# A decoder layer on one core: x and memory also come transposed from the host, factors are applied on the way out

## The chip, the cores and the metric

The kernel runs on one core of a Trainium2 chip. The metric is device time in microseconds (us) of one execution. All arithmetic is in float32; matmuls run on operands split in two parts (hi, lo), so that each product is three matmuls.

## The reference, cut to what matters

One layer of a causal decoder: 1024 tokens of width 1024 (x) and 256 memory tokens of width 1024 (mem). The change touches the two norms at the start and what is made from them:

```python
def rms_norm(x, w):
    y = x * lax.rsqrt(jnp.mean(x * x, axis=-1, keepdims=True) + EPS)
    return y * w

h = rms_norm(x, norm_mix_w)
x = x + hybrid_mixer(h, w_in, pool_w, ...)       # one input projection h @ w_in, two head groups, w_out
h = rms_norm(x, norm_xattn_w)
m = rms_norm(mem, norm_mem_w)
x = x + memory_cross_attention(h, m, wq, wkv, wo) # kv = m @ wkv; k = kv[:, :1024], v = kv[:, 1024:]
h = rms_norm(x, norm_ffn_w)
x = x + conv_ffn(h, w_up, conv_w, conv_b, w_down) # depthwise convolution of width 3, SwiGLU
return rms_norm(x, norm_final_w)
```

The factor of a row (the rsqrt) and the factor of a feature (w) are separate, so that a projection of the unnormalised rows can be multiplied by the row's factor afterwards.

## The kernel before, in words

**Tiling.** Matmuls contract over 128 features at a time, so activations must lie feature-major (features on the partitions). `Feat` (line 230) holds an activation so, in tiles of hi and lo parts; `split` (line 94) makes both: ScalarE writes hi (line 96), VectorE the rest (line 97). Rows come from HBM token-major, are normalised there and transposed by TensorE against an identity, 128x128 at a time (`put_T`, line 302, matmuls of line 307). `norm_feat` (line 312) does that for four tiles of 128 tokens, a block of 512; there are two blocks.

**Norms.** `inv_rms` (line 290) takes the square sum of a row tile on ScalarE (line 292) and the power -0.5 on GpSimd (line 294); `normed` (line 297) multiplies tile, factor and the broadcast norm vector on VectorE (line 299).

**Weights.** Each weight chunk is 512 KB, loaded by SP (`dma`, line 273) and split in two units (`wunit`, lines 117 and 118). A stream takes the units in the order of the jobs, two units ahead. The 16 chunks of the memory projection wkv go to roomy buffers of the pool "big" (40 buffers), so that they can be loaded early; all others go through two raw buffers.

**Jobs.** Matmul work is a list of jobs in fixed order: km (K of memory, 8 blocks of 128 features, each 8 x 3 matmuls 128x256), vm (V of memory, 96 matmuls 128x512), then for each block vg, k, q, r, p, and wout. `fill` runs steps of the first open job for a planned number of us; `weave` runs a chain, such as norm_feat, and fills between its steps. What a chain issues and what jobs issue is ordered for each engine by the program's order and by a planner's estimate of when operands are ready, except for pinned instructions: these stay behind what was traced before them on their engine. All loads by SP are pinned until job vm is done; so are the splits of weights at the start.

**The start** (lines 496 to 523): memory's two row tiles are loaded first, with its norm vector, which TensorE broadcasts with a row of ones (line 502) for the product of line 509; then weight chunks and the four row tiles of x alternate; memory's tiles are transposed. While km and vm run, the first block of x is normalised and transposed, and `make_vec` (line 561) transposes the packed convolution and scale vectors, which five small loads brought (lines 548 to 552). The second block's norm_feat runs beside the output projection of the first (job wout).

Of the kernel before, what the change touches and what calls it, by code (L numbers as in the profile page):

```python
# [8 lines left out]
F32 = mybir.dt.float32  # L9
F32R = mybir.dt.float32r  # L10
AF = mybir.ActivationFunctionType
ALU = mybir.AluOpType
# [3 lines left out]
P = 128  # L16
T = 1024
D = 1024
KT = D // P
TB = 512  # L20
NB = T // TB
M = 256
# [5 lines left out]
HK = KT // 2  # L28
# [11 lines left out]


@with_exitstack
def hybrid_layer(ctx: ExitStack, tc: tile.TileContext, x, mem, norm_mix_w, w_in, pool_w, pool_scale,
                 gk_w2, gk_b, gla_norm_w, w_out, norm_xattn_w, norm_mem_w, wq, wkv, wo,
                 norm_ffn_w, w_up, conv_w, conv_b, w_down, norm_final_w, out):
    nc = tc.nc

    const = ctx.enter_context(tc.tile_pool(name="const", bufs=1))
# [9 lines left out]
    pin = tc.keep_in_program_order  # L58
# [3 lines left out]
    def nm(s):  # L62
        uid[0] += 1
        return f"{s}{uid[0]}"

    def f4(*shape):
        return big.tile([P, *shape], F32, tag="big", name=nm("f"))

    def r4(*shape):
        return big.tile([P, *shape], F32R, tag="big", name=nm("r"))  # L70
# [4 lines left out]
    def sc(n):  # L75
        return small.tile([P, n], F32, tag="small", name=nm("s"))

    def bankA():
        return psA.tile([P, 512], F32, tag="psA", name=nm("pa"))

    def bankB():
        return psB.tile([P, 512], F32, tag="psB", name=nm("pb"))
# [11 lines left out]
    def split(dst, src, scale=None):  # L94
        if scale is None:
            nc.scalar.activation(dst.hi, src, AF.Copy)  # L96
            nc.vector.tensor_tensor(dst.lo, src, dst.hi.bitcast(F32), ALU.subtract)  # L97
        else:
            nc.scalar.activation(dst.hi, src, AF.Copy, scale=scale)
            nc.vector.scalar_tensor_tensor(dst.lo, src, scale, dst.hi.bitcast(F32), ALU.mult, ALU.subtract)  # L100
# [41 lines left out]
    early, issues = [False], []  # L142
# [19 lines left out]
    ws = Stream()  # L162
# [34 lines left out]
    def fill(us):  # L197
        while us > 0:
            c = step()
            if c is None:  # L200
                return
            us -= c
# [6 lines left out]
    def weave(chain):  # L209
        for us in chain:  # L210
            fill(us)
# [8 lines left out]
    def proj_tok(banks, feat, nk, step_k, n):  # L220
        for kc in range(0, nk, step_k // 2):
            w = ws.take()
            for i, ps in enumerate(banks):
                for kk in range(step_k // 2):
                    a = feat.k(kc + kk)
                    mm3(ps, a[:, i * P:(i + 1) * P], w[:, kk, :], kc + kk == 0, kc + kk == nk - 1)
                    yield n * 3 / 2400
# [40 lines left out]
    ident = const.tile([P, P], F32, name="ident")  # L268
# [4 lines left out]
    def dma(dst, src):  # L273
        ins = nc.sync.dma_start(out=dst, in_=src)
        if starting or pinned:
            pin(ins)

    def bcast_row(src, q=nc.gpsimd):
        w = f4(D)
        ins = q.dma_start(out=w, in_=src.partition_broadcast(P))  # L280
        if starting:
            pin(ins)
        return w

    def load_x(t):
        xt = f4(D)
        dma(xt, x[t * P:(t + 1) * P, :])
        return xt

    def inv_rms(xt, junk):  # L290
        ss, rs = sc(1), sc(1)
        nc.scalar.activation(junk, xt, AF.Square, scale=1.0 / 32, accum_out=ss)
        nc.gpsimd.tensor_scalar(ss, ss, EPS, None, ALU.add)
        nc.gpsimd.tensor_tensor(rs, ss, halfneg[:, 0:1], ALU.pow)
        return rs

    def normed(xt, wb, pool=None):
        y = pool.tile([P, D], F32, tag="y", name=nm("y")) if pool else f4(D)
        nc.vector.scalar_tensor_tensor(y, xt, inv_rms(xt, y), wb, ALU.mult, ALU.mult)
        return y  # L300

    def put_T(xn, feat, c0):
        pss = []
        for q in range(2):
            ps = bankB()
            for j in range(4):
                nc.tensor.transpose(ps[:, j * P:(j + 1) * P], xn[:, (4 * q + j) * P:(4 * q + j + 1) * P], ident)  # L307
            pss.append(ps.rearrange("p (k c) -> p k c", k=4))
            feat.put(4 * q, 4, c0, P, pss[q])
        return pss  # L310

    def norm_feat(tiles, wb, feat, lead=6.0):

        ahead = normed(tiles[0](), wb)
        yield lead
        for i in range(len(tiles)):
            xn = ahead
            if i + 1 < len(tiles):
                ahead = normed(tiles[i + 1](), wb)
            put_T(xn, feat, i * P)  # L320
            yield 5.0

    hmix = [None, None]
# [80 lines left out]
    tiles = [0]  # L404
# [34 lines left out]
    att = {}  # L439

    def kmem_evac(f, ps):
        if f == 0:
            att["K"] = Feat(M)
        att["K"].put(f, 1, 0, M, ps.unsqueeze(1))

    def vmem_gen():
        V = att["V"] = [Pair(r4(D), r4(D)) for _ in range(2)]
        for half in range(2):
            banks = [bankA() for _ in range(2)]
            yield from proj_tok(banks, att["m"], KT, 2, 512)  # L450
            for i in range(2):
                split(V[i][:, half * 512:(half + 1) * 512], banks[i])

    hx, oo = [None, None], [None, None]

# [29 lines left out]
    def allow(*keys):  # L485
        for k in keys:
            J[k].open = True


    def load_m(i):  # L490
        mt = f4(D)
        dma(mt, mem[i * P:(i + 1) * P, :])
        return mt

    ones, row = f4(P), f4(D)
    nc.vector.memset(ones[0:1, :], 1.0)
    mts = [load_m(0)]
    dma(row[0:1, :], norm_mem_w.rearrange("(o c) -> o c", o=1))
    mts.append(load_m(1))
    wb_mem = [bankA(), bankA()]  # L500
    for half in range(2):
        nc.tensor.matmul(wb_mem[half], ones[0:1, :], row[0:1, half * 512:(half + 1) * 512], start=True, stop=True)
    att["m"] = Feat(M)
    xn = [f4(D), f4(D)]
    for xt, y in zip(mts, xn):
        rs = inv_rms(xt, y)
        for half in range(2):
            hs = slice(half * 512, (half + 1) * 512)
            pin(nc.vector.scalar_tensor_tensor(y[:, hs], xt[:, hs], rs, wb_mem[half], ALU.mult, ALU.mult))
    for k in range(2):  # L510
        issues[k]()
    ws.load(1)
    xts = [load_x(0)]
    wb_mix = bcast_row(norm_mix_w, nc.sync)
    for i in range(1, 4):
        issues[i + 1]()
        xts.append(load_x(i))
    put_T(xn[0], att["m"], 0)
    ws.load(2)
    put_T(xn[1], att["m"], P)  # L520
    ws.load(2)
    hmix[0] = Feat(TB)


# [7 lines left out]
                            fill=0.0, base=0, channel_multiplier=1)  # L532
# [10 lines left out]
    phalo = mixc.tile([P, 4, HALO], F32, name="phalo")  # L543
    pin(nc.gpsimd.memset(phalo, 0.0))

    rows_a = f4(P)
    rows_b = f4(P)
    pin(nc.sync.dma_start(out=rows_a[0:88, :], in_=conv_w[0:2, :].rearrange("w (f p) -> (w f) p", p=P)))
    pin(nc.sync.dma_start(out=rows_b[0:44, :], in_=conv_w[2, :].rearrange("(f p) -> f p", p=P)))
    pin(nc.sync.dma_start(out=rows_b[44:88, :], in_=conv_b.rearrange("(f p) -> f p", p=P)))  # L550
    pin(nc.sync.dma_start(out=rows_b[88:92, :], in_=pool_scale.rearrange("(f p) -> f p", p=P)))
    pin(nc.sync.dma_start(out=rows_b[92:93, :], in_=gla_norm_w.rearrange("(f p) -> f p", p=P)))
    gkw = mixc.tile([17, 256], F32, name="gkw")
    pin(nc.sync.dma_start(out=gkw[0:16, :], in_=gk_w2))
    pin(nc.sync.dma_start(out=gkw[16:17, :], in_=gk_b.rearrange("(o c) -> o c", o=1)))
    poolw = mixc.tile([P, 4, P], F32, name="poolw")
    pin(nc.sync.dma_start(out=poolw, in_=pool_w.rearrange("g c d -> c g d")))

    vec = const.tile([P, 181], F32, name="vec")

    def make_vec():
        ps = bankB()
        nc.tensor.transpose(ps[:, 0:88], rows_a[0:88, :], ident[0:88, 0:88])
        nc.tensor.transpose(ps[:, 88:181], rows_b[0:93, :], ident[0:93, 0:93])
        nc.vector.tensor_copy(vec, ps[:, 0:181])

    def cw(j, f):
        return vec[:, j * 44 + f:j * 44 + f + 1]
# [129 lines left out]

    starting.clear()
    allow("km", "vm")  # L700
    weave(norm_feat([lambda i=i: xts[i] for i in range(4)], wb_mix, hmix[0], 5.0))
    make_vec()
    finish(J["vm"])
    pinned.clear()
    mixs[0] = Feat(TB)
# [5 lines left out]
    J["wout", 0, 0].limit = None  # L711
    allow(("wout", 0, 0), ("wout", 0, 512))
    hmix[1] = Feat(TB)
    weave(norm_feat([lambda i=i: load_x(4 + i) for i in range(4)], wb_mix, hmix[1]))
    finish(J["q", 1])
    mixs[1] = Feat(TB)
    allow(("r", 1), ("p", 1))
# [162 lines left out]
    for i in range(4):  # L880
# [4 lines left out]
        xn = normed(xres[4 + i], wb_f, ybuf)  # L885
# [302 lines left out]
    for j in list(plan):  # L1188
# [4 lines left out]
    finish(plan[0])  # L1193


_INS = ["x", "mem", "norm_mix_w", "w_in", "pool_w", "pool_scale", "gk_w2", "gk_b", "gla_norm_w", "w_out",
        "norm_xattn_w", "norm_mem_w", "xattn_wq", "xattn_wkv", "xattn_wo", "norm_ffn_w", "ffn_w_up",
        "ffn_conv_w", "ffn_conv_b", "ffn_w_down", "norm_final_w"]


# [18 lines left out]
```

## Time and profile before

| | |
|---|---|
| median of 3 runs | 1299.7 us (1299.69 to 1301.9) |
| profiled execution, its own time | 1303.83 us |
| its span, first to last instruction | 1300.4 us |
| mean granted TensorE clock | 0.994 |
| VectorE busy | 862.9 us (66%) |
| ScalarE busy | 648.7 us (50%) |
| GpSimd busy | 227.7 us (18%) |
| DMA moved | 143.94 MB, mean 111 GB/s |

PE is TensorE's matmuls, PEld its weight loads, DVE VectorE, ACT ScalarE, POOL GpSimd, SPq the sequencer that issues most loads. Matmuls overlap, so the distance between two starts says what one costs in the queue, and the duration says more than that. A tile is named by its variable: `f` and `r` are buffers of the pool "big", `wr`, `wh`, `wl` a raw weight chunk and its two parts, `pa` and `pb` PSUM banks.

### The profile page before, as it was taken

What the parts mean: (1) busy time and instruction counts of PE and PEld (TensorE: products, weight loads), DVE (VectorE), ACT (ScalarE), POOL (GpSimd) and SP (SyncE); (2) the same over time, 40 slices, a digit from 0 to 9 for tenths busy, and PEclk for the clock granted to TensorE, in tenths of its full rate; (3) what the DMA queues carried; (4) which work ended last, traced back from release to release, by engine and by line L of the source; (5) the groups of instructions that cost most, each with busy time, mean ns of one, the idle gap of its engine ahead of it and who ended that gap; (6) DMA issues with size and microseconds to landing.
All of it is one profiled execution on the core that took longest, in us unless ns stands there. A gap on an engine that the chain in (4) does not pass through costs nothing.

```text
span 1300.4 us, 16897 instructions
## 1 busy us (share of the span) xinstructions
PE 1269.9 (98%) x6326; PEld 1059.7 (81%) x6326; DVE 862.9 (66%) x1331; ACT 648.7 (50%) x1169; POOL 227.7 (18%) x238
## 2 busy tenths in 40 slices
PE   8999999999999999999899999999999999999997
PEld 7898878988788889887777888888888886888885
DVE  6723676236757554446887667668667678999865
ACT  6636534364445443335555555545545544474453
POOL 2000110001200000010114443434434420000002
PEclk9999999999999999999999999999999999999999
DMA  9433225332142212233323232232232246875202
GB/s 288 144 101 82 66 98 196 99 81 66 63 148 65 66 52 79 72 117 127 121 68 99 79 98 75 72 98 81 65 97 82 65 149 238 286 249 187 81 22 107
DMA packets 140272, 143.94 MB, mean 111 GB/s; under 512 B 4696, under 2 KB 112926, under 8 KB 140191
## 3 DMA queue, kind: packets, MB, share of 16 engines
q1 hardware_dynamic: 138031, 136.05, 32.5%
q0 software_dynamic: 1584, 5.77, 1.2%
q8 instruction: 49, 0.80, 0.3%
q10 hardware_dynamic: 576, 1.05, 0.2%
q14 instruction: 32, 0.26, 0.1%
HBM read 122.93 MB, written 19.92 MB: 110 GB/s over the span
## 4 chain that ended last, share of the span: by engine, by line
PE 67%; issue 16%; DVE 7%; DMA 4%; ACT 3%; POOL 1%; SPq 0%; POOLq 0%; ACTq 0%; DVEq 0%
PE pa L913 8%; PE pa L914 8%; PE pa L915 8%; PE pa L92 8%; PE pa L90 8%; PE pa L91 8%; PE pb L913 5%; PE pb L914 5%; PE pb L915 5%; DVE r L97 2%; DMA f<-gd 2%; DVE wl L118 1%; PE pb L307 1%; DMA f<-in_norm_ffn_w_dram 1%; DVE wl L97 1%
## 5 line engine op out<-in xcount | busy, mean ns | idle before, releaser
L118 DVE TENSOR_TENSOR wl<-wr,wh 128x512 fp32r<-128x512 f32 (+1 forms) x222 | 152.9, 691 | 208.7 <-ACT wh L117 203.7
L117 ACT ACTIVATE wh<-wr 128x512 fp32r<-128x512 f32 (+1 forms) x222 | 140.0, 632 | 282.9 <-PE pa L91 82.1
L913 PE MATMUL pa<-r,wh 128*128 128x512 f32 x400 | 158.8, 397 | 7.5 <-ACT wh L117 4.5
L90 PE MATMUL pa<-wh,r 128*128 128x512 f32 (+2 forms) x480 | 159.2, 332 | 0.3 <-ACT wh L117 0.3
L915 PE MATMUL pa<-r,wl 128*128 128x512 f32 x400 | 158.6, 397 | 0.0
L914 PE MATMUL pa<-r,wh 128*128 128x512 f32 x400 | 158.4, 396 | 0.0
L91 PE MATMUL pa<-wl,r 128*128 128x512 f32 (+2 forms) x480 | 157.3, 328 | 0.3 <-DVE wl L118 0.3
L92 PE MATMUL pa<-wh,r 128*128 128x512 f32 (+2 forms) x480 | 157.0, 327 | 0.2
L90 PE MATMUL pa<-r,wh 128*128 128x512 f32 (+1 forms) x384 | 149.3, 389 | 0.7 <-ACT r L96 0.7
L92 PE MATMUL pa<-r,wl 128*128 128x512 f32 (+1 forms) x384 | 144.2, 376 | 0.4 <-DVE wl L118 0.3
L91 PE MATMUL pa<-r,wh 128*128 128x512 f32 (+1 forms) x384 | 144.0, 375 | 0.3 <-DVE r L97 0.3
L92 PEld LDWEIGHTS pa<-wh,r 128*128 128x128 f32 x480 | 90.3, 188 | 9.4 <-DVE r L97 1.1
L913 PEld LDWEIGHTS pa<-r,wh 128*128 128x128 f32 x400 | 75.9, 190 | 26.5 <-ACT wh L117 4.7
L90 PEld LDWEIGHTS pa<-wh,r 128*128 128x128 f32 x480 | 90.4, 188 | 8.3 <-ACT wh L117 0.5
L91 PEld LDWEIGHTS pa<-wl,r 128*128 128x128 f32 x480 | 90.4, 188 | 8.2 <-DVE wl L118 0.5
L981 DVE SCALAR_TENSOR_TENSOR f<-f,vec,f 128x1023 f32<-128x1023 f32 x44 | 86.9, 1974 | 14.5 <-ACT f L980 14.5
L915 PEld LDWEIGHTS pa<-r,wl 128*128 128x128 f32 x400 | 75.8, 190 | 17.7 <-DVE wl L118 0.4
L914 PEld LDWEIGHTS pa<-r,wh 128*128 128x128 f32 x400 | 75.9, 190 | 17.0
L117 ACT ACTIVATE wh<-ws 128x512 fp32r<-128x512 f32 x88 | 55.4, 630 | 67.9 <-PE pa L914 33.6
L913 PE MATMUL pb<-r,wh 128*128 128x512 f32 x216 | 85.1, 394 | 0.0
L914 PE MATMUL pb<-r,wh 128*128 128x512 f32 x216 | 85.0, 394 | 0.0
L915 PE MATMUL pb<-r,wl 128*128 128x512 f32 x216 | 84.7, 392 | 0.0
(225 smaller groups left out, 2660.9 us busy)
## 6 DMA issues: line engine op xcount, KB each, us to landing
wr<-in_ffn_w_up_dram SPq DMA_DIRECT2D x47, 512.0 KB, 3.7
wr<-in_ffn_w_down_dram SPq DMA_DIRECT2D x33, 512.0 KB, 3.7
wr<-in_w_in_dram SPq DMA_DIRECT2D x24, 512.0 KB, 4.0
gd<-f SPq DMA_DIRECT2D x22, 512.0 KB, 2.6
f<-gd SPq DMA_DIRECT2D x22, 512.0 KB, 5.8
f<-in_xattn_wkv_dram SPq DMA_DIRECT2D x16, 512.0 KB, 7.6
f<-in_x_dram SPq DMA_DIRECT2D x16, 512.0 KB, 7.6
wr<-in_w_out_dram SPq DMA_DIRECT2D x16, 512.0 KB, 3.6
```

What stands on the lines that cost most here:

```text
L90: nc.tensor.matmul(ps, l.hi, r.hi, start=start, stop=False)
L91: nc.tensor.matmul(ps, l.hi, r.lo, start=False, stop=False)
L92: nc.tensor.matmul(ps, l.lo, r.hi, start=False, stop=stop)
L97: nc.vector.tensor_tensor(dst.lo, src, dst.hi.bitcast(F32), ALU.subtract)
L117: ia = nc.scalar.activation(w.hi, src, AF.Copy)
L118: ib = nc.vector.tensor_tensor(w.lo, src, w.hi.bitcast(F32), ALU.subtract)
L307: nc.tensor.transpose(ps[:, j * P:(j + 1) * P], xn[:, (4 * q + j) * P:(4 * q + j + 1) * P], ident)
L913: nc.tensor.matmul(ps, l.hi, r.hi, start=start, stop=False, **kw)
L914: nc.tensor.matmul(ps, l.hi, r.lo, start=False, stop=False, **kw)
L915: nc.tensor.matmul(ps, l.lo, r.hi, start=False, stop=stop, **kw)
L981: nc.vector.scalar_tensor_tensor(v[:, 1:], u[:, 0:T - 1], cw(1, f), v[:, 1:], ALU.mult, ALU.add)
```

## The change

The host gives three more arrays: x transposed, mem transposed, and `vecs`, in which the convolution and scale vectors and the two norm vectors norm_mix_w and norm_mem_w lie ready as 197 columns of 128 features. The rows of x and mem are still loaded, for their square sums.

- Memory: its transposed features (two loads of 512 KB) are multiplied by norm_mem_w while they are split. K and V are projected from these unnormalised features. V is multiplied by the row factor when it leaves PSUM; for K the factors are a row vector across the free axis, made by `spread_cols` (a column spread over 128 columns, transposed by TensorE), and K's evacuation multiplies by it. K's blocks that are done before this row exists wait in their banks (`att["wait"]`).
- x: `mix_rows` replaces norm_feat in both blocks. It takes the square sums of four row tiles, loads the block's transposed half (four loads of 512 KB), spreads the four factors, multiplies features by norm vector and factors on VectorE, and splits.
- Order at the start: the vectors by ScalarE's queue, then by SP weight chunk 0, memory transposed, weight chunks 1 and 2, memory's rows alternating with chunks 3 and 4, x's row tiles with chunks 5 to 7.

```diff
-        att["K"].put(f, 1, 0, M, ps.unsqueeze(1))
+        def close():
+            k = t2(M)
+            nc.vector.tensor_tensor(k, ps, att["rs"], ALU.mult)
+            att["K"].put(f, 1, 0, M, k.unsqueeze(1))
+        if att["wait"] is None:
+            close()
+        else:
+            att["wait"].append(close)
...
-                split(V[i][:, half * 512:(half + 1) * 512], banks[i])
+                split(V[i][:, half * 512:(half + 1) * 512], banks[i], att["rsm"][i])
...
+    vec = const.tile([P, 197], F32, name="vec")
+    def spread_cols(rs, dst):
+        ps = bankB()
+        for i, r in enumerate(rs):
+            o = t2(P)
+            nc.vector.tensor_scalar(o, ident, 0.0, r, ALU.mult, ALU.add)
+            nc.tensor.transpose(ps[:, i * P:(i + 1) * P], o, ident)
+        nc.scalar.activation(dst, ps[:, 0:P * len(rs)], AF.Copy)
+    def by_features(src, c0, n):
+        ts = []
+        for j in range(0, KT, 1024 // n):
+            t = f4(1024 // n, n)
+            dma(t, src[j * P:(j + 1024 // n) * P, c0:c0 + n].rearrange("(k p) c -> p k c", p=P))
+            ts.append(t)
+        return lambda k: ts[k * n // 1024][:, k % (1024 // n), :]
+    pin(nc.scalar.dma_start(out=vec, in_=vecs))
+    issues[0]()
+    mT = by_features(memT, 0, M)
+    for k in (1, 2):
+        issues[k]()
     mts = [load_m(0)]
-    dma(row[0:1, :], norm_mem_w.rearrange("(o c) -> o c", o=1))
+    issues[3]()
     mts.append(load_m(1))
-    wb_mem = [bankA(), bankA()]
-    for half in range(2):
-        nc.tensor.matmul(wb_mem[half], ones[0:1, :], row[0:1, half * 512:(half + 1) * 512], start=True, stop=True)
+    issues[4]()
+    xts = [load_x(0)]
+    issues[5]()
+    xts.append(load_x(1))
+    issues[6]()
+    xts.append(load_x(2))
+    issues[7]()
+    xts.append(load_x(3))
     att["m"] = Feat(M)
...
+    for h in range(2):
+        ws.load(h + 1)
+        for k in range(HK * h, HK * h + HK):
+            att["m"].put(k, 1, 0, M, mT(k).unsqueeze(1), wmem(k))
+    rsm = att["rsm"] = [inv_rms(t, f4(D)) for t in mts]
+    att["rs"], att["wait"] = f4(M), []
+    def mix_rows(b, tiles):
+        rs = [inv_rms(t(), f4(D)) for t in tiles]
+        xb = by_features(xT, b * TB, TB)
+        yield 6.0
+        rsx = f4(TB)
+        spread_cols(rs, rsx)
+        yield 2.0
+        for k in range(KT):
+            t = t2(TB)
+            nc.vector.scalar_tensor_tensor(t, xb(k), wmix(k), rsx, ALU.mult, ALU.mult)
+            split(hmix[b].k(k), t)
+            yield 1.5
...
-    weave(norm_feat([lambda i=i: xts[i] for i in range(4)], wb_mix, hmix[0], 5.0))
-    make_vec()
+    fill(10.5)
+    spread_cols(rsm, att["rs"])
+    for c in att["wait"]:
+        c()
+    att["wait"] = None
+    weave(mix_rows(0, [lambda i=i: xts[i] for i in range(4)]))
...
-    weave(norm_feat([lambda i=i: load_x(4 + i) for i in range(4)], wb_mix, hmix[1]))
+    weave(mix_rows(1, [lambda i=i: load_x(4 + i) for i in range(4)]))
...
+    given["xT"], given["memT"] = given["x"].T, given["mem"].T
+    given["vecs"] = _np.concatenate([given[k].reshape(-1, P).T for k in (
+        "ffn_conv_w", "ffn_conv_b", "pool_scale", "gla_norm_w", "norm_mix_w", "norm_mem_w")], axis=1)
```

## Rows read from the trace of the kernel before

**Rows 1.** The page's first part: each engine's busy time, share of span, instructions.
```profile
PE 1269.9 (98%) x6326; PEld 1059.7 (81%) x6326; DVE 862.9 (66%) x1331; ACT 648.7 (50%) x1169; POOL 227.7 (18%) x238
```

**Rows 2.** Stretches of the head: length, busy time (instructions), granted clock, DMA share, GB/s.
```profile
2.00:20.00 18.00, 14.14 (x75) 10.48 (x76) 11.06 (x17) 11.34 (x23) 5.62 (x33) 1.00 1.05 337
20.00:24.00 4.00, 4.00 (x37) 4.00 (x36) 3.23 (x7) 2.13 (x6) 0.81 (x2) 1.00 0.37 120
24.00:30.00 6.00, 5.97 (x52) 5.77 (x52) 5.14 (x11) 4.74 (x12) 0.79 (x2) 1.00 1.11 305
30.00:40.00 10.00, 9.42 (x78) 9.01 (x79) 8.83 (x19) 7.54 (x19) 0.79 (x2) 1.00 1.05 386
```

**Rows 3.** PE in order of time: start, duration, line, operation, count, idle before.
```profile
12.08 0.39 PE L90 MATMUL pa<-r,wh 128*128 128x256 f32 x1 [0.69 <-ACT r L96]
...
40.87 0.48 PE L90 MATMUL pa<-wh,r 128*128 128x512 f32 x1
...
63.20 0.39 PE L92 MATMUL pa<-wh,r 128*128 128x512 f32 x1
63.42 0.28 PE L90 MATMUL pa<-wh,r 128*128 128x264 f32 x1
```

**Rows 4.** ACT in order of time, first uses of the second and third load.
```profile
6.57 1.06 ACT L292 ACTIVATE f<-f 128x1024 f32<-128x1024 f32 x1 [0.90 <-DMA f<-in_mem_dram]
...
8.36 0.63 ACT L117 ACTIVATE wh<-f 128x512 fp32r<-128x512 f32 x1 [0.64 <-DMA f<-in_xattn_wkv_dram]
```

**Rows 5.** SP's issues in order of time.
```profile
18.78 0.32 SPq L554 DMA_DIRECT2D gkw<-in_gk_w_dram  x1
...
22.09 0.40 SPq L557 DMA_DIRECT2D poolw<-in_pool_w_dram  x1
22.53 9.27 SPq L274 DMA_DIRECT2D f<-in_xattn_wkv_dram  x11
```

**Rows 6.** PE in order of time around eight transposes.
```profile
25.66 0.28 PE L92 MATMUL pa<-r,wl 128*128 128x256 f32 x1
25.78 1.04 PE L307 MATMUL pb<-ident,f 128*128 128x128 f32 x8
26.57 0.36 PE L90 MATMUL pa<-r,wh 128*128 128x256 f32 x1
26.77 0.28 PE L91 MATMUL pa<-r,wh 128*128 128x256 f32 x1
```

**Rows 7.** The transposes' line over the span: duration in ns least/median/most, first and last start.
```profile
L307 PE MATMUL pb<-ident,f x144: 270/273/477, 8.5 to 410.7; 128*128 128x128 f32 x144
```

**Rows 8.** DVE groups of the first 63 us: busy us, mean ns, idle before.
```profile
L118 DVE TENSOR_TENSOR wl<-f,wh 128x512 fp32r<-128x512 f32 x32 | 21.4, 687 | 5.4 <-ACT wh L117 5.2
L97 DVE TENSOR_TENSOR r<-pb,r 128x256 fp32r<-128x256 f32 x16 | 6.4, 418 | 0.1
L299 DVE SCALAR_TENSOR_TENSOR f<-f,s,f 128x1024 f32<-128x1024 f32 x4 | 5.1, 1285 | 3.4 <-POOL s L294 3.4
L509 DVE SCALAR_TENSOR_TENSOR f<-f,s,pa 128x512 f32<-128x512 f32 x4 | 2.8, 745 | 6.8 <-PE pa L502 6.8
```

**Rows 9.** POOL in order of time, the last factor of the first block.
```profile
31.86 0.57 POOL L294 TENSOR_TENSOR s<-s,halfneg 128x1 f32<-128x1 f32 x1
```

**Rows 10.** Stretches around a stop of TensorE, same columns as before.
```profile
642.00:646.00 4.00, 0.00 (x0) 0.00 (x0) 4.00 (x10) 2.77 (x8) 0.00 (x0) 1.00 0.44 131
646.00:650.00 4.00, 3.96 (x10) 2.86 (x11) 4.00 (x10) 4.00 (x12) 0.00 (x0) 0.58 0.33 93
650.00:654.00 4.00, 4.00 (x19) 3.23 (x18) 3.79 (x10) 2.05 (x5) 0.00 (x0) 1.00 0.57 171
```

**Rows 11.** SP's issues in order of time, second block.
```profile
191.19 5.50 SPq L274 DMA_DIRECT2D wr<-in_w_out_dram  x2
196.74 2.55 SPq L274 DMA_DIRECT2D f<-in_x_dram  x5
202.75 0.38 SPq L274 DMA_DIRECT2D wr<-in_w_out_dram  x1
```

**Rows 12.** SP's waits from 170 to 260 us: total, times, longest.
```profile
SPq L274 <- DVE r L97: 15.0, 2, 8.9
```

More of the change, by code (lines that the diff above doesn't have):

```diff
@@ L42, in hybrid_layer @@
 @with_exitstack
-def hybrid_layer(ctx: ExitStack, tc: tile.TileContext, x, mem, norm_mix_w, w_in, pool_w, pool_scale,
-                 gk_w2, gk_b, gla_norm_w, w_out, norm_xattn_w, norm_mem_w, wq, wkv, wo,
-                 norm_ffn_w, w_up, conv_w, conv_b, w_down, norm_final_w, out):
+def hybrid_layer(ctx: ExitStack, tc: tile.TileContext, x, mem, w_in, pool_w, gk_w2, gk_b, w_out, norm_xattn_w,
+                 wq, wkv, wo, norm_ffn_w, w_up, w_down, norm_final_w, xT, memT, vecs, out):
     nc = tc.nc
@@ L493, in load_m, with wmix, wmem @@
         return mt
-    ones, row = f4(P), f4(D)
-    nc.vector.memset(ones[0:1, :], 1.0)
+    vec = const.tile([P, 197], F32, name="vec")
+    def wmix(k):
+        return vec[:, 181 + k:182 + k]
+    def wmem(k):
+        return vec[:, 189 + k:190 + k]
+    def spread_cols(rs, dst):
[5 more added lines that the diff above has]
+        nc.scalar.activation(dst, ps[:, 0:P * len(rs)], AF.Copy)
@@ L499, in hybrid_layer @@
     mts.append(load_m(1))
-    wb_mem = [bankA(), bankA()]
-    for half in range(2):
-        nc.tensor.matmul(wb_mem[half], ones[0:1, :], row[0:1, half * 512:(half + 1) * 512], start=True, stop=True)
-    att["m"] = Feat(M)
[L504 to L521, printed above, removed]
+    issues[4]()
[6 more added lines that the diff above has]
+    xts.append(load_x(3))
+    att["m"] = Feat(M)
@@ L544, in hybrid_layer @@
     pin(nc.gpsimd.memset(phalo, 0.0))
[L546 to L552, printed above, removed]
     gkw = mixc.tile([17, 256], F32, name="gkw")
@@ L557, in hybrid_layer @@
     pin(nc.sync.dma_start(out=poolw, in_=pool_w.rearrange("g c d -> c g d")))
[L559 to L565, printed above, removed]
     def cw(j, f):
@@ L1193, in hybrid_layer @@
     finish(plan[0])
-_INS = ["x", "mem", "norm_mix_w", "w_in", "pool_w", "pool_scale", "gk_w2", "gk_b", "gla_norm_w", "w_out",
-        "norm_xattn_w", "norm_mem_w", "xattn_wq", "xattn_wkv", "xattn_wo", "norm_ffn_w", "ffn_w_up",
-        "ffn_conv_w", "ffn_conv_b", "ffn_w_down", "norm_final_w"]
+_INS = ["x", "mem", "w_in", "pool_w", "gk_w2", "gk_b", "w_out", "norm_xattn_w", "xattn_wq", "xattn_wkv", "xattn_wo",
+        "norm_ffn_w", "ffn_w_up", "ffn_w_down", "norm_final_w", "xT", "memT", "vecs"]
 def kernel(**inputs):
@@ L1206 @@
     nc = _bacc.Bacc("TRN2", target_bir_lowering=False, num_devices=1)
+    given = {k: _np.asarray(v) if k == "norm_final_w" else _np.asarray(v)[0] for k, v in inputs.items()}
+    given["xT"], given["memT"] = given["x"].T, given["mem"].T
+    given["vecs"] = _np.concatenate([given[k].reshape(-1, P).T for k in (
+        "ffn_conv_w", "ffn_conv_b", "pool_scale", "gla_norm_w", "norm_mix_w", "norm_mem_w")], axis=1)
     arrays, args = {}, []
     for name in _INS:
-        a = _np.ascontiguousarray(inputs[name])
-        if name != "norm_final_w":
-            a = a.reshape(a.shape[1:])
+        a = _np.ascontiguousarray(given[name])
         arrays[f"in_{name}_dram"] = a
```

## The prediction

> **What bounds the kernel now.** I read the page first: TensorE is busy 98% of a span of 1300.4 us [rows 1], so a change is worth what it takes out of TensorE's queue, or what it adds to that engine's waits. Then I read the table of stretches, for the stage that the change rebuilds, the first 63 us. There the DMA engines are full from 2 to 20 us (337 GB/s), slacken to 120 GB/s from 20 to 24, and are full again (305, then 386 GB/s) until 40 [rows 2]. TensorE's order of time says what this stage is: the first matmul of the K projection (job km) issues at 12.08, the first of the V projection (job vm) at 40.87, the first of the next job, vg, at 63.42 [rows 3]. From 12.08 on the engine hardly waits. So before, the head is 12 us of waiting for memory, its normalisation and its transposes, and then 51 us of packed TensorE work. What follows is bound by TensorE too, so a microsecond gained at 63.42 should last to the end, unless it is lost again on the way.
>
> **Part 1, transposes.** Removed: 16 of memory, 32 of x in the first block, 32 in the second, 2 for the vectors. Added: 2 and 4 and 4, in spread_cols. What is one worth? Eight of them stand between the matmul at 25.66 and that at 26.57; without them the next matmul would have come 0.12 us later, so eight cost 0.91 - 0.12 = 0.79 us, with a little more behind them (the second matmul comes 0.20 later, not 0.12): 0.87 in all, 0.11 each. The group's row gives each a duration of 273 ns, but they overlap [rows 6, 7]. The Trainium skill's page "TensorE: Matmul & The Clock Gate" (section "Part 4: PE-mode transpose") puts a 128x128 transpose at about 275 ns in a kernel's context; as a duration this trace agrees, as time in the queue it does not, and the difference is a rival below. In the second block the engine is packed and nothing else bounds it, so 28 x 0.11 = 3.1 us come off. In the first block the saving counts only if TensorE bounds there afterwards.
>
> **Part 2, the start.** Memory came first in the queue, and TensorE waited for its load, two broadcasts by matmul, the square sums, the product and the transposes. Afterwards the first weight chunk comes first, then memory's two transposed halves; the packed vectors (0.10 MB) go beside them. Landing: memory's second half MB (1.05 MB in all) was first used at 6.57 and the first weight chunk (1.57 MB) at 8.36. At 337 GB/s from 2.0 us these bytes take until 5.1 and 6.7, so add about 1.5 us [rows 2, 4]. Vectors, weight chunk and first half of memory are 1.15 MB: 2.0 + 3.4 + 1.5 = 6.9 us, and 0.4 for the first split: TensorE begins at 7.3 instead of 12.08. The first column block is paced by the splits of memory (eight of 128x256 by VectorE, 0.42 each [rows 8], and two of weights) and ends near 11; seven more at 24 matmuls x 0.118 = 2.8 us end at 31. The last weight chunk of K is there at 2.0 + 7.96 MB / 337 + 1.5 = 27.1, early enough. K's close now waits for the factor row, which comes from memory's rows (second half behind 4.7 MB: 17.5 us, and some 3 us of sums and spreading). Four banks wait for it, a fifth is being filled, and the sixth column block starts near 22: cover of 2 us, and if it failed, there is slack at 31 anyway, as follows.
>
> **Part 3, the bytes.** SP issues loads in the order of the program, and this decides. Before, the eight V chunks were issued from 22.53 to 31.8 and were there long before TensorE came to them at 40.87. Now ahead of the first V chunk stand: vectors 0.10, K weights 4.19, memory twice 2.10, x 2.10, the gate and pool weights 0.28, and, new, the first block's four loads of transposed x, 2.10: with the V chunk itself 11.39 MB. Gone are the 0.52 MB broadcast of a norm vector and five tiny loads, in whose place the queue had run dry: SP's next issues wait until 18.78 and 22.09 [rows 5], which is the 120 GB/s of rows 2. The first 8.77 MB at 337 GB/s take from 2.0 to 28.0, the last 2.62 MB at 386 GB/s until 34.8; 1.5 us to landing and 0.6 for the first split: TensorE can begin V at 36.9. It has finished K at 31 and stands still for nearly 6 us: the plan has no other job for it.
>
> **Part 4, what the wait costs beyond itself.** Rows show what a stop does here: after 4.0 us without a matmul from 642 to 646 the granted clock is 0.58 over the next 4 us (full is 2.4 GHz, the other level 1.2), and 1.00 again after that [rows 10]: 0.42 x 4 = 1.7 us lost. I take 1.7. Below, zero (if K runs later, so that the stop is short); above, 1.7 and the next item.
>
> **Part 5, VectorE.** Before, x cost it per block four products of 1.28 and eight subtractions of 0.69; now eight products of about 0.75 and the same subtractions: 11.5 us instead of 10.6, with the small spreads. But they cannot begin before the last rows of x have landed (28.8 us by the same sum), been squared (1.1), gone through GpSimd (0.6 [rows 9] and as much again for handing over) and been spread: about 33. From 33 until V's last weight unit is due (57), VectorE owes 11.5 + 16 x 0.687 (V's units) + 1.5 = 24 us [rows 8]. It just fits, but not evenly: in the first microseconds of V, products of x and weight units alternate, 2.4 us of VectorE for units that TensorE eats in 1.6. Bounds: nothing (while the clock is low, TensorE eats more slowly) to 3 us; I take 0.6, since most of it lies under the low clock. ScalarE does as many splits as before and fewer transposed evacuations, and has room. V's evacuation gains a factor, 0.745 for 0.687, four times: nothing.
>
> **Sum.** V takes 63.42 - 40.87 = 22.5 us. Afterwards 36.9 + 22.5 + 1.7 + 0.6 = 61.7 instead of 63.4: 1.7 us gained at the head, though TensorE starts 5 us earlier and has 50 transposes fewer. With the second block 4.8 us. Against the profiled execution's own span that is 1295.6 of 1300.4, and with the 3.4 us around it 1299.0 of 1303.8; the runs' median of 1299.7 lies 4.1 under that execution, so I carry the difference over: **1294.9 us**.
>
> **Rivals.**
> (a) The loads come faster, and TensorE never stops long. If all 11.39 MB came at 386 GB/s, V could begin at 2.0 + 29.5 + 1.5 + 0.6 = 33.6; no low clock, 0.5 for VectorE: 56.6, a gain of 6.8, with 3.1 makes 1289.8. For it: the V chunks and the transposed x are read in runs of 2 KB, and the fast stretch is the one with V chunks. Against it: K's weight chunks, with runs of 512 bytes, are a third of the bytes, and the stretch of the last three of them gives 305 GB/s [rows 2].
> (b) The head's gain is eaten. At 305 GB/s throughout, V begins at 2.0 + 37.3 + 2.1 = 41.4, and with 1.7 and 0.6 ends at 66.2: 2.8 us lost, 3.1 gained later: 1299.4. VectorE's upper bound of 3 us instead of 0.6 moves the forecast the same way, to 1297.3.
> (c) Slower. In the second block SP issues four loads of x rows and four of transposed x, in whose buffers older tiles still lie. Before, SP waited up to 8.9 us for such a buffer, 15.0 in two waits [rows 12], and issued up to five of these loads in a row in front of an output weight chunk [rows 11]. If the transposed loads wait so, the weight chunks behind them are late: 8.9 for the buffer and 4 x 0.524 MB / 386 = 5.4 of transfer, less the 5.6 us that one chunk in hand covers (24 matmuls x 0.234), is a stop of 8.7, and 1.7 of low clock: 1294.9 + 10.4 = 1305.3. It decides from the point at which the queue's delay passes those 5.6 us; at half the wait it is 1300. Against it: a row tile is free again as soon as its square sum is taken, where before it lay until the product.
> (d) Each transpose costs its whole duration in the queue, as the page's figure would have it: 28 x 0.273 = 7.6 instead of 3.1 in the second block: 1290.4. The spacing in rows 6 speaks against it.
>
> **Chances.** Forecast (1292 to 1297) 0.50; (a) 0.13; (d) 0.03; (b) 0.20; (c) 0.14. What this kernel's measurement can tell from no change is 0.2%, 2.6 us. Faster than 1297.1: the forecast, (a) and (d), 0.66. Within: (b) but for 0.03, and 0.03 of (c): 0.20. Slower than 1302.3: the rest, 0.14. The range runs from (a) at its fast end, 1289.3, through (b) to where (c) begins to count as slower, 1302.0.
>
> **What would show it.** In the changed kernel's trace: the first K matmul near 7; the last near 31; a stop of TensorE of about 6 us before the first matmul of V, ended by a split that had waited for a load, and a granted clock near 0.5 behind it; no dip in the DMA rate around 20; vg's first matmul near 61.7; in the second block 4 transposes instead of 32 and no wait of TensorE for weights. The forecast is wrong if V begins at 31 to 33 (the order or the rate of the loads was misjudged), if vg begins after 64, or if the stretch of the second block holds a stop.

## The result, and the profile after

The changed kernel is slower: 1309.28 us (1307.53 to 1312.54, 4 runs) beside 1300.41 for the kernel before in the same runs, ratio 1.007 with an interval of 1.0047 to 1.0092, some 9 us (6 to 12). The forecast was 1294.9, and the range ended at 1302.0. The profiled execution has 1307.53 us of its own and a span of 1305.8; that of before lay 3.4 above its median (1303.83, span 1300.4), so the two spans differ by 5.4 only.

The page's first part, whose row of before is [rows 1]: 76 matmuls fewer and 9 us less of busy TensorE, in a longer span. The engine waits instead of working.

```profile
PE 1260.7 (97%) x6250; PEld 1053.5 (81%) x6250; DVE 866.6 (66%) x1339; ACT 649.7 (50%) x1160; POOL 226.3 (17%) x238
```

TensorE's order of time, where it answers to [rows 3] (start, duration, line, what it does, count, and in brackets the idle time before and what ended it):

```profile
7.79 0.58 PE L89 MATMUL pa<-r,wh 128*128 128x256 f32 x1 [7.79 <-ACT r L98]
...
16.08 0.47 PE L518 MATMUL pb<-ident,t 128*128 128x128 f32 x1 [2.83 <-DVE t L517]
...
41.95 0.73 PE L89 MATMUL pa<-wh,r 128*128 128x512 f32 x2 [2.19 <-ACT wh L116]
43.84 0.79 PE L90 MATMUL pa<-wl,r 128*128 128x512 f32 x1 [1.16 <-DVE wl L117]
...
67.10 0.28 PE L89 MATMUL pa<-wh,r 128*128 128x264 f32 x1
...
212.81 0.80 PE L89 MATMUL pa<-wh,r 128*128 128x512 f32 x1 [5.10 <-DVE f L434]
```

K starts at 7.79, 4.3 us earlier than before. But there is a stop ahead of 16.08, K's last matmul issues at 39.49 (before: 40.40), V begins at 41.95 instead of 40.87, and vg at 67.10 instead of 63.42: 3.7 us lost at the head. A stop of 5.1 us in the second block loses about as much again. The stretches (length, busy time and instructions of PE, PEld, DVE, ACT and POOL, granted clock, DMA share, GB/s) belong to [rows 2]:

```profile
2.00:12.00 10.00, 4.21 (x18) 3.98 (x19) 4.65 (x10) 4.98 (x11) 0.00 (x0) 1.00 1.10 301
12.00:20.00 8.00, 5.17 (x27) 4.85 (x27) 2.06 (x5) 4.89 (x9) 2.52 (x10) 0.79 1.12 339
20.00:30.00 10.00, 10.00 (x87) 10.00 (x87) 7.23 (x15) 5.48 (x12) 2.59 (x21) 1.00 1.10 344
30.00:40.00 10.00, 8.89 (x72) 8.14 (x70) 7.67 (x19) 7.76 (x16) 4.87 (x8) 1.00 1.05 386
40.00:50.00 10.00, 6.89 (x23) 5.25 (x24) 10.00 (x18) 6.89 (x13) 0.00 (x0) 0.83 0.89 315
50.00:60.00 10.00, 10.00 (x45) 8.12 (x44) 9.19 (x15) 6.75 (x12) 0.00 (x0) 1.00 0.00 0
...
200.00:220.00 20.00, 14.22 (x52) 10.46 (x52) 14.70 (x24) 8.40 (x15) 1.53 (x3) 0.83 0.69 267
```

The loads do what was forecast: no dip at 20 us, 344 and 386 GB/s. What is new is VectorE, busy for 10.0 of 10 us from 40 to 50 while TensorE works 6.89.

**Where the head stops.** In these traces an instruction of ScalarE or VectorE that waits holds up those queued behind it. ScalarE around 13 us:

```profile
9.36 1.69 ACT L98 ACTIVATE r<-f,vec 128x256 fp32r<-128x256 f32 x4
13.59 1.06 ACT L291 ACTIVATE f<-f 128x1024 f32<-128x1024 f32 x1 [2.54 <-DMA f<-in_mem_dram]
14.55 0.19 ACT L291 ACTIVATION_READ_ACCUMULATOR f<-f 128x1 f32 x1
14.64 0.61 ACT L116 ACTIVATE wh<-f 128x512 fp32r<-128x512 f32 x1
```

It has nothing to do from 11.05 to 13.59 because the square sum of memory's first row tile stands ahead of the split of a weight chunk whose load was issued before that tile's. VectorE repeats it:

```profile
10.09 1.66 DVE L99 SCALAR_TENSOR_TENSOR r<-f,vec,r 128x256 fp32r<-128x256 f32 x4
15.73 0.29 DVE L517 TENSOR_SCALAR t<-ident,s 128x128 f32<-128x128 f32 x1 [3.98 <-POOL s L293]
15.94 0.69 DVE L117 TENSOR_TENSOR wl<-f,wh 128x512 fp32r<-128x512 f32 x1
```

The spread of memory's row factor (L517) waits 3.98 us for GpSimd's power, and the weight split L117 behind it waits along. TensorE has used up its weights by then. It is the same ahead of V: ScalarE's split of the first weight units for V comes at 41.29, without a wait for a load, behind x's last square sum (34.47), the copy of x's spread factors (37.61) and the first splits of x (39.03, 40.03).

**Where the second block stops.** SP's issues there, in order of time:

```profile
194.97 2.18 SPq L273 DMA_DIRECT2D f<-in_xT_dram  x4
199.51 0.37 SPq L273 DMA_DIRECT2D wr<-in_w_out_dram  x1
199.97 1.86 SPq L273 DMA_DIRECT2D f<-in_x_dram  x4
```

and VectorE:

```profile
209.42 2.73 DVE L563 SCALAR_TENSOR_TENSOR t<-f,vec,f 128x512 f32<-128x512 f32 x4
212.07 0.68 DVE L434 TENSOR_TENSOR f<-pa,f 128x512 f32<-128x512 f32 x1
```

Ahead of 212.81 TensorE waits for a PSUM bank. The residual add of L434 frees it, at 212.07; it needs a row tile of x that is loaded a second time (issued from 199.97), and in the queue 2.1 MB of transposed x stand before it. The first of these tiles had landed at about 209.1 (9.1 us after its issue), 1.4 us into the stop. The add came 3 us later, because it stands also behind four products of x on VectorE, from 209.42 to 212.15.

### The profile page after: what moved, and what is told of

The parts are those of the page before. It is cut to its first block, busy times and chain, and to the rows that moved or that the text cites. A ratio compares the mean times of both kernels' runs of the same rounds, so it can differ in the third digit from the quotient of the medians.

```text
span 1305.8 us, 16733 instructions
## 1 busy us (share of the span) xinstructions
PE 1260.7 (97%) x6250; PEld 1053.5 (81%) x6250; DVE 866.6 (66%) x1339; ACT 649.7 (50%) x1160; POOL 226.3 (17%) x238
## 4 chain that ended last, share of the span: by engine, by line
PE 71%; issue 16%; DVE 5%; DMA 3%; ACT 3%; POOL 1%; SPq 0%; POOLq 0%; ACTq 0%; DVEq 0%
PE pa L947 9%; PE pa L948 9%; PE pa L949 9%; PE pa L89 8%; PE pa L90 8%; PE pa L91 8%; PE pb L947 5%; PE pb L948 5%; PE pb L949 5%; DMA f<-gd 1%; DVE r L96 1%; POOL s L293 1%; DMA f<-in_mem_dram 1%; DMA f<-in_norm_ffn_w_dram 1%; DVE t L563 1%
## 5 line engine op out<-in xcount | busy, mean ns | idle before, releaser
L117 DVE TENSOR_TENSOR wl<-wr,wh 128x512 fp32r<-128x512 f32 (+1 forms) x222 | 154.0, 696 | 209.9 <-ACT wh L116 204.8
L89 PE MATMUL pa<-r,wh 128*128 128x512 f32 (+1 forms) x384 | 151.1, 393 | 7.8 <-ACT r L98 7.8
L90 PE MATMUL pa<-r,wh 128*128 128x512 f32 (+1 forms) x384 | 145.6, 379 | 0.0
L947 PEld LDWEIGHTS pa<-r,wh 128*128 128x128 f32 x400 | 75.6, 189 | 26.8 <-ACT wh L116 4.9
L89 PEld LDWEIGHTS pa<-r,wh 128*128 128x128 f32 x384 | 74.2, 193 | 21.4 <-ACT r L98 7.8
L949 PEld LDWEIGHTS pa<-r,wl 128*128 128x128 f32 x400 | 75.5, 189 | 17.7 <-DVE wl L117 0.4
L948 PEld LDWEIGHTS pa<-r,wh 128*128 128x128 f32 x400 | 75.6, 189 | 16.8
L91 PEld LDWEIGHTS pa<-r,wl 128*128 128x128 f32 x384 | 73.7, 192 | 14.1
L948 PE MATMUL pb<-r,wh 128*128 128x512 f32 x216 | 85.0, 393 | 0.0
```

The lines of the kernel that those rows point to most:

```text
L89: nc.tensor.matmul(ps, l.hi, r.hi, start=start, stop=False)
L90: nc.tensor.matmul(ps, l.hi, r.lo, start=False, stop=False)
L91: nc.tensor.matmul(ps, l.lo, r.hi, start=False, stop=stop)
L117: ib = nc.vector.tensor_tensor(w.lo, src, w.hi.bitcast(F32), ALU.subtract)
L947: nc.tensor.matmul(ps, l.hi, r.hi, start=start, stop=False, **kw)
L948: nc.tensor.matmul(ps, l.hi, r.lo, start=False, stop=False, **kw)
```

## The experiments

Two theories at this point. Head: weight splits stand behind work on row factors and on x in in-order queues. Second block: the reload of the residual rows stands behind the transposed x, and the adds behind the products of x. Every kernel below was run 5 to 11 times beside the kernel before in the same batch (medians there 1300.64 to 1301.55).

**The changed head alone** (second block by the old norm_feat):

```diff
-    weave(mix_rows(1, [lambda i=i: load_x(4 + i) for i in range(4)]))
+    wb_mix = bcast_row(norm_mix_w)
+    weave(norm_feat([lambda i=i: load_x(4 + i) for i in range(4)], wb_mix, hmix[1]))
```

> The changed start, but the second block normalised and transposed as before. Theory: two separate losses, +3.7 us at the first vg matmul (67.1 against 63.4) and +3.9 in the second block (a stop of 5.1 us and 2 us of low clock, less 3.1 us of transposes). Then this kernel is 3.5 to 4 us slower than the one before, and some 4 faster than the changed one; TensorE does not wait for the residual adds of the first output half. Rival: the stop in the second block only follows from the head's shift of 3.7 us in time; then it stays here and this kernel is 6 us or more slower than the one before.

1304.38 us, ratio 1.0032 (1.0019 to 1.0044). No stop in the second block (TensorE 19.74 of the 20 us from 200). The head costs about 4 us.

**The changed second block alone** (everything else as before; mix_rows, spread_cols, by_features and the transposed x for block 1):

```diff
-    weave(norm_feat([lambda i=i: load_x(4 + i) for i in range(4)], wb_mix, hmix[1]))
+    weave(mix_rows(1, [lambda i=i: load_x(4 + i) for i in range(4)]))
```

> The start as before, only the second block by transposed x. Theory: the stop for the residual adds (about 5 us, and 2 of low clock) is there without the changed head: 3.5 to 4 us slower than before. Rival, as predicted: the second block gains its 28 transposes, 3.1 us faster than before.

1304.73 us, ratio 1.0033 (1.002 to 1.0045). The stop is there without the changed head; TensorE's waits from 200 to 220 (what for: total, times, longest):

```profile
PE pa L90 <- DVE f L435: 5.1, 1, 5.1
```

The two parts, 4.2 and 4.3 us by their ratios (each within 1.6), add up to 8.5 of the 9 of the whole change.

**The transposed x behind the residual rows.**

```diff
         rs = [inv_rms(t(), f4(D)) for t in tiles]
+        if b:
+            yield 11.0
         xb = by_features(xT, b * TB, TB)
-        yield 6.0
+        yield 4.0 if b else 6.0
```

(and the later yields of the second block 1.0 and 1.2 instead of 2.0 and 1.5.)

> The changed kernel, but in the second block the four loads of transposed x are issued after the reload of the residual rows, and its steps are spaced accordingly. Theory: what stops TensorE is that the residual adds, which free the banks, come late, because their rows are loaded behind the transposed ones and the products stand ahead of them on VectorE. Then the stop and the low clock go and the 3.1 us of transposes remain: 7 us faster than the changed kernel, about 0.5 us slower than the one before. Rival: VectorE has too much to do in this stretch in any order; then at least half of the stop stays, at another place.

1301.46 us, ratio 1.0006 (0.9997 to 1.0015). This kernel's SP queue:

```profile
195.39 2.50 SPq L273 DMA_DIRECT2D f<-in_x_dram  x5
197.99 3.08 SPq L273 DMA_DIRECT2D f<-in_xT_dram  x4
```

and its stretch:

```profile
200.00:220.00 20.00, 19.24 (x86) 15.29 (x85) 12.50 (x21) 8.25 (x14) 1.53 (x3) 1.00 0.74 283
```

The four residual tiles now go first, the stop is gone, TensorE works 19.24 of 20 us at full clock instead of 14.22 at 0.83. So the order of the work makes the second block's loss. Two things moved at once, though: the loads, and the products of x on VectorE, which now begin at 211.92, behind the adds (203.68 to 207.73). How much each is worth is not shown; the 1.4 and 3 us of the changed kernel's stop are the nearest. The run also prices the transposes: this kernel and the changed head alone differ in the second block only, with 28 transposes fewer here and no long stop in either: 1304.38 - 1301.46 = 2.9 us (1.4 to 5.4 by the two intervals), net of whatever else differs there, such as a wait of 0.76 us at 217.78 here.

**Memory's spread: only TensorE's order.** The two transposes of memory's factors pinned, so that TensorE does not take them ahead of matmuls.

```diff
-            nc.tensor.transpose(ps[:, i * P:(i + 1) * P], o, ident)
+            tr = nc.tensor.transpose(ps[:, i * P:(i + 1) * P], o, ident)
+            if keep:
+                pin(tr)
```

> The changed kernel, with the first of the two small transposes that spread memory's row factors moved behind the fifth column block of K in TensorE's queue, where the program has it; nothing else in any queue differs. Theory: the stop of 2.8 us at 13 us, the low clock behind it (1.4 us) go, K ends near 35.5 instead of 39.6, and V begins 2 to 3.5 us earlier: the whole is 2 to 3.5 us faster than the changed kernel. Rival: V's start hangs on something else than K's end (its first weight split stands behind the products of x on ScalarE and VectorE); then K ends earlier, V begins at 41 to 42 all the same and the time is the changed kernel's within 0.5 us.

1308.58 us, ratio 1.0063 (1.0049 to 1.0076): as the whole change. TensorE no longer waits for L517, but for what stands behind it in the other queues:

```profile
15.32 0.39 PE L89 MATMUL pa<-r,wh 128*128 128x256 f32 x1 [1.73 <-ACT wh L116]
16.69 0.39 PE L91 MATMUL pa<-r,wl 128*128 128x256 f32 x1 [0.87 <-DVE wl L117]
```

So the transposes' place in TensorE's queue was not the cause; the releaser of the first trace was only the last to come.

**Memory's square sums behind the weight splits** (on top of the late transposed x, as all that follow).

```diff
-    rsm = att["rsm"] = [inv_rms(t, f4(D)) for t in mts]
...
-    fill(10.5)
-    spread_cols(rsm, att["rs"])
+    fill(5.1)
+    rsm = att["rsm"] = [inv_rms(t, f4(D), True) for t in mts]
+    fill(5.4)
+    spread_cols(rsm, att["rs"], True)
```

> late_xt, and memory's row factors taken later: their square sums are traced two column blocks after the start, and they, the spread columns and the small transposes are pinned behind the weight splits traced before them on their engines. Theory: the stop at 13 us is ScalarE waiting at a square sum for memory's rows, and VectorE at a spread column for the factor, both with the next weight chunk's split behind them, though that chunk is there. With the splits ahead of them the second column block follows the first at 13.2 instead of 16.2, the low clock behind the stop goes, K ends near 35.3 and V begins at 38 to 39: 3 to 3.5 us faster than late_xt. Rival: V's start is set by the products of x ahead of its first split; then K ends early, V begins at 41 or later, and less than 1 us is gained.

1298.47 us, ratio 0.9984 (0.9976 to 0.9993): 3.0 less than without it, and the first version faster than before. The stop at 13 is gone, K's last matmul comes at 37.65 instead of 39.49. V's start, however:

```profile
40.11 0.73 PE L89 MATMUL pa<-wh,r 128*128 128x512 f32 x2 [2.19 <-ACT wh L116]
42.01 0.79 PE L90 MATMUL pa<-wl,r 128*128 128x512 f32 x1 [1.16 <-DVE wl L117]
```

The same waits as in the changed kernel, 1.84 us earlier and not shorter: what V waits for here is the chain of x, which came earlier too, and not a load. The first V chunk had landed at about 38.1, and its split came at 39.45.

**The work on x later.** In the first block 9.0 instead of 6.0 us of TensorE's work before x's spread, and 2.2 instead of 1.5 between products: with the late transposed x alone, and on top of the last one.

```diff
-        yield 4.0 if b else 6.0
+        yield 4.0 if b else 9.0
...
-            yield 1.2 if b else 1.5
+            yield 1.2 if b else 2.2
```

> late_xt, and the first block's spreading, products and splits of x spaced out over job vm (steps of 9.0 and 2.2 instead of 6.0 and 1.5 planned us). Theory of the head's stop at 13 us: K still ends near 39.6, so V gains only what its first splits stood behind products: 0.5 to 1 us faster than late_xt. Rival (the products of x set V's start): 3 us or more faster.

> units_first and late_mix together. Theory: K ends near 35.3; the first V chunk lands at 37, behind the four loads of transposed x; V begins at 37.7 to 38.5: 3.5 to 4.5 us faster than late_xt, and TensorE still stops 2 to 3 us at V's start, at a split that waits for a load. Rival (loads don't matter): V begins right at 35.5.

1304.11 us (ratio 1.0022, 1.0012 to 1.0032) in the first case, 2.7 more than without it; 1301.46 (1.0005, 0.9996 to 1.0014) in the second, 3.0 more than the moved square sums without it. Both miss. The later spread only lengthened the wait at V's start, as the weight splits stayed behind it. In the second case K's last matmul issued at 35.67 and the first V chunk landed at about 38.1, so there some 2.4 us of the wait are the load's in any case. In the first case, TensorE's row and the stretches:

```profile
43.02 1.22 PE L89 MATMUL pa<-wh,r 128*128 128x512 f32 x2 [4.36 <-ACT wh L116]
```
```profile
42.00:46.00 4.00, 2.25 (x5) 1.33 (x6) 4.00 (x7) 3.57 (x7) 0.00 (x0) 0.50 1.05 379
46.00:50.00 4.00, 4.00 (x11) 3.13 (x10) 3.86 (x7) 0.98 (x2) 0.00 (x0) 0.50 0.62 205
50.00:54.00 4.00, 4.00 (x17) 3.19 (x16) 2.85 (x5) 1.54 (x3) 0.00 (x0) 0.85 0.00 0
```

Here the clock stays at 0.50, the lower level, for 8 us. That is not a matter of the stop's length. In the second case the waits were the same, 4.36 and 0.73, and full pace (matmuls 0.23 us apart instead of 0.43) was back at 45.32, 5.0 us after V's first matmul:

```profile
40.31 1.22 PE L89 MATMUL pa<-wh,r 128*128 128x512 f32 x2 [4.36 <-ACT wh L116]
...
45.32 0.39 PE L89 MATMUL pa<-wh,r 128*128 128x512 f32 x1
```

In the changed head alone waits of 2.15 and 1.16 went with half pace for 8.0 us, in the changed kernel waits of 2.19 and 1.16 with 5.0. The clock of the changed head alone, beside 0.83 in the changed kernel:

```profile
40.00:50.00 10.00, 7.02 (x17) 5.27 (x18) 10.00 (x18) 6.51 (x12) 0.00 (x0) 0.66 0.89 314
```

**Four chunks of V ahead of the transposed x**, on top of both.

```diff
+        if not b:
+            for k in range(8, 12):
+                issues[k]()
         xb = by_features(xT, b * TB, TB)
```

> both, with the first four V chunks issued ahead of the four loads of transposed x. Theory: the bytes ahead of V are what is left, so the stop at V's start goes: V begins within 0.5 us of K's end, near 35.5, no low clock there; 2.5 to 4 us faster than both, 6 to 8 faster than late_xt, which makes 1294 to 1295 beside 1300.6 for the kernel before. Rival: the products of x then come too late, and vg waits for them at 58 to 62; nothing is gained over both.

1299.69 us, ratio 0.9991 (0.9982 to 1.0), 1.8 less than without it, where 2.5 to 4 were expected. V follows K at 35.83 without a wait, but the stop comes back later:

```profile
50.64 1.22 PE L89 MATMUL pa<-wh,r 128*128 128x512 f32 x2 [3.53 <-ACT wh L116]
53.24 0.80 PE L90 MATMUL pa<-wl,r 128*128 128x512 f32 x1 [1.38 <-DVE wl L117]
```

ScalarE's order of time shows why: between 44.64 and 49.97 it splits x five times, with waits for VectorE's products (0.37 to 0.72), and evacuates twice, before the next weight split. The earlier loads also brought V's first weight splits ahead of the splits of x in ScalarE's queue (34.73 to 41.59), so which of the two let V follow K is not shown. The rest is the order of the splits from 44 on.

**Weight splits and splits of x in turn.** As the last one, with spread and products at 6.0 and 2.4 us, and all splits of x and of V's weights pinned in program order.

```diff
-        if starting:
+        if starting or pacing:
...
+                d = hmix[b].k(k)
+                pin(nc.scalar.activation(d.hi, t, AF.Copy))
+                pin(nc.vector.tensor_tensor(d.lo, t, d.hi.bitcast(F32), ALU.subtract))
```

(The first condition pins a weight unit; `pacing` holds from x's first product to V's end.)

> As both_v (memory's square sums behind its weight splits, the first four chunks of V's weights issued ahead of the transposed x), with the work on x in the first block spaced differently: x spread at 6.0 instead of 9.0, a product every 2.4 us of TensorE's work, and from the first product to V's end the splits of x and the splits of V's weight chunks placed in program order, so that they alternate in ScalarE's and VectorE's queues instead of standing in bunches. Theory (in-order queues): V begins at about 36 at K's end as in both_v, the stops of 3.5 and 1.4 us between 50 and 54 shrink to under 1.5 together, TensorE's clock stays full in 50 to 60, vg begins at 61 to 63 instead of 65.5, and the time is 1295 to 1297.5. Rival: VectorE has more to do between K's end and vg than there is room for (10.0 of 10 us busy in 40 to 50 in the changed kernel), whatever the order: stops of 4 us or more stay somewhere ahead of vg, vg begins at 65 to 66.5, and the time is 1299 to 1301.

1296.38 us (1296.1 to 1297.08, 5 runs), ratio 0.9964 (0.9952 to 0.9977): 4.7 us faster than before by the ratio, 13 faster than the change as it was made. TensorE around V, and the stretches:

```profile
36.97 0.63 PE L89 MATMUL pa<-wh,r 128*128 128x512 f32 x2
...
39.34 0.73 PE L89 MATMUL pa<-wh,r 128*128 128x512 f32 x2 [0.83 <-ACT wh L116]
40.70 0.50 PE L90 MATMUL pa<-wl,r 128*128 128x512 f32 x1 [0.62 <-DVE wl L117]
...
62.13 0.28 PE L89 MATMUL pa<-wh,r 128*128 128x264 f32 x1
```
```profile
40.00:50.00 10.00, 9.04 (x39) 7.00 (x39) 10.00 (x18) 6.07 (x12) 0.00 (x0) 1.00 0.86 307
50.00:60.00 10.00, 9.94 (x43) 7.77 (x42) 9.55 (x16) 7.37 (x13) 0.00 (x0) 1.00 0.00 0
```

VectorE is as full as in the changed kernel (10.00 and 9.55 of 10), and TensorE works 9.04 and 9.94 at full clock where it worked 6.89 and 10.00 at 0.83 and 1.00. The same work in another order: the rival, too much work for VectorE, is out. The step from the last kernel, 3.3 us, changed the spacing and the order of the splits together; their shares were not taken apart.

**A warm start.** In the changed kernel the first column block is spaced at 0.21 us a matmul until 12.7, and then at 0.12. Before, the matmuls that spread memory's norm row ran ahead of K. That they make the difference is doubtful: with the changed second block alone they ran too, from 4.42, and the matmuls of K were 0.21 apart from 13.1 to 16.3, with 1.00 in the clock column and 52 matmuls in 8 us where the kernel before had 59:

```profile
12.00:20.00 8.00, 8.00 (x52) 8.00 (x52) 6.82 (x11) 6.04 (x12) 0.85 (x2) 1.00 1.10 338
```

Here 24 products of the identity with itself run on TensorE first:

```diff
+    heat = bankB()
+    for i in range(24):
+        nc.tensor.matmul(heat[:, 0:P], ident, ident, start=True, stop=True)
```

> As units_first, with 24 multiplications of the identity by itself (128x128, float32, output not used) put ahead of everything on TensorE while the first loads are under way. Theory: the first column block of K is slow (0.214 a matmul, about 5 us to 12.7) only because nothing ran on TensorE ahead of it; in the kernel before, the matmuls that spread the memory's norm row ran from 4.8 to 8.6 and did that work. With TensorE busy from about 1.5 to 7 the first 24 K matmuls are spaced at 0.11 and take 2.8 us, the second block of K follows at 10.5 instead of 12.7 (or waits for its weights, at most 1.5 us), and all that follows on TensorE comes 1 to 2 us earlier: 1296.5 to 1297.5 beside 1298.5 of units_first. Rival 1: the start of V hangs on the row factors and products of x, which come no earlier, so that TensorE only waits longer ahead of V: K's end moves by 1 to 2 us, V's first matmul stays at 40 and the time stays at 1298.5. Rival 2: the spacing is set by something else than the clock and stays at 0.214: no change anywhere.

> paced with the 24 multiplications of the identity ahead of everything on TensorE. Theory: their gain of 1 to 2 us comes on top of paced's, since V there starts at K's end and not at the work on x: 1294 to 1296, vg at 60 to 62. Rival: the chunks of V's weights land no earlier (bytes bound it: the first at about 37, later ones in their order), so that an earlier end of K only becomes a stop ahead of V: same as paced within 0.7 us.

1301.27 us with the square sums moved (ratio 0.9999, 0.9991 to 1.0008), 2.8 more than without the products; 1297.02 on top of the last kernel (0.997, 0.9959 to 0.9982), 0.6 more, within the intervals. Both miss: a loss in the first case, no gain in the second. The spacing did become 0.12 from the first matmuls on (TensorE of the first of the two):

```profile
8.75 0.28 PE L92 MATMUL pa<-r,wl 128*128 128x256 f32 x1
8.87 0.28 PE L90 MATMUL pa<-r,wh 128*128 128x256 f32 x1
...
24.58 0.52 PE L521 MATMUL pb<-ident,t 128*128 128x128 f32 x2 [2.90 <-DVE t L520]
```

But K began later, at 8.43 instead of 8.01 and at 9.34 instead of 7.57, as the products ran until then. TensorE still got ahead and stopped for 2.9 us, until 24.58: the spread of memory's factors stands on VectorE behind a weight split, and that split's first half on ScalarE behind a load:

```profile
22.97 1.15 ACT L117 ACTIVATE wh<-f 128x512 fp32r<-128x512 f32 x2 [1.93 <-DMA f<-in_xattn_wkv_dram]
```

So here the loads do bind, and in the stretch 24 to 30 of the second of the two the clock is at 0.50. K's last matmul issued at 38.23 instead of 37.65, and at 38.83 instead of 36.85: more than was gained is given back. That it would pay with the spread placed later was not tried.

## Why the prediction was wrong

**Right.** K starts at 7.79 (7.3 in Part 2), no dip in the loads, and of Part 1 the second block's 28 transposes: 2.9 us net by the experiment (1.4 to 5.4), 3.1 in the sum. Rival (d), each transpose at its whole duration, asked 7.6 and is excluded here. The Trainium skill gives that duration as about 275 ns ("TensorE: Matmul & The Clock Gate", "Part 4: PE-mode transpose"); this case's 273 ns agree, and they are not the price in the queue. The bytes of Part 3 hold roughly: the stretches' rates came as reckoned, and the first V chunk landed at about 37.9 (issued at 30.26, 7.6 us to landing) instead of 36.3. But its split came at 41.29, so the bytes did not set V's start.

**The step that failed first: Part 2**, "cover of 2 us, and if it failed, there is slack at 31 anyway". I asked when TensorE would need the factor row, not what stands behind the instruction that waits for it. What was late was not the row but the weight splits behind square sum and spread, on ScalarE and VectorE. K then ended at 39.5 instead of 31: the stop (2.8), the half pace after it (until 19.4, where 3.3 us did the work of 1.7), and the first column block at half pace (5.3 us where the sum had 3.7 for the splits of memory) come to 6.0 of the 8.5; the start's 0.5 and further small waits are the rest. The slack of 6 us in which the forecast hid all this was gone. Moving the square sums gave 3.0 of it back.

**Part 5**, "It just fits, but not evenly", with 0.6 taken of 0 to 3. The amount was right (VectorE full for 10 us), and the loss was not in the amount: with the order as made, V began at 41.95, 2.5 us behind K's end, stood still once more and ran at half clock to 46.9, and vg came at 67.10 instead of 61.7. With the same work in turn, and the square sums and four V chunks in their new places, vg came at 62.13. The order in the queues, not throughput, set the price, and the bounds that I had drawn by throughput were too near.

**The second block**, in the sum a plain gain of 3.1. Rival (c) had the place, the queue of SP where x and transposed x are loaded, and a price of 10.4; but it looked at a buffer's wait and at weight chunks as victims. The victims were the residual reload and the adds that need it, behind transposed x in the queue of SP and behind its products on VectorE; of both the prediction said nothing, though it had counted such a queue for the head in Part 3; 4.3 lost there and 2.9 of transposes that did not show make 7.2 for the stop of 5.1 and the low clock behind it (with the loads in the other order the time fell by 1309.28 - 1301.46 = 7.8).

**Which case it was.** By time the nearest is (c), 1305.3, at a chance of 0.14, together with the eaten head of (b); as neither's mechanism came about, the nearness is luck. The forecast's test "if V begins at 31 to 33, if vg begins after 64, or if the second block holds a stop" hit with the last two. That about 4.2 belong to the head and 4.3 to the second block is shown, and that the order of the work in the engines' queues, with that of the loads, makes both losses. What each wait costs by itself was not taken apart.

## What to carry to other kernels

When a chain is moved or added, list for every engine it touches what stands behind its waiting instruction, above all splits that feed TensorE, and for the load queue every later load, reloads too. Slack on the bounding engine is only as good as the order of the queues that feed it: with work alternated instead of bunched, and the loads in another order, the same change went from 1309.3 to 1296.4 us here. After a stop, add the low clock: behind V's start it was 5 to 8 us of half pace here, after waits of some 2 and of some 4 us alike.

## What the runs showed of the hardware that I had not expected

- TensorE's first matmuls in the changed kernel run at half pace, 0.21 us apart for the first 5 us, and 0.12 apart when 24 products of the identity had run ahead of them. The clock column reads 1.00 over that stretch (2 to 12 in the rows above), so it does not show this; the spacing does. Matmuls ahead do not always prevent it: with the changed second block alone norm matmuls and transposes ran ahead of K, and it had 0.21 from 13.1 to 16.3 all the same. What decides is open.
- How long the half pace lasts after a stop does not follow from the stop's length: counted from V's first matmul, it was 5.0 us (changed kernel) and 8.0 (changed head alone) with waits of some 2.2 and 1.2 us; 5.0 (square sums moved and work on x later) and 8.1 (work on x later alone) with 4.36 and 0.73.
- 28 transposes fewer in a packed TensorE queue were worth 2.9 us net, some 0.1 each, though each lasts 270 ns in the trace [rows 7].
